# Expert results combined by one-hot products on TensorE instead of a round trip through DRAM, and the second branch's gate projections moved beside the first attention

## The chip, the cores and the metric

The kernel runs on one NeuronCore of a Trainium2 chip. The metric is the device time of one execution in microseconds (us), lower is better; 0.2% of it is about 4.4 us. PE is the matrix engine (TensorE), PEld its weight loads, DVE the vector engine, ACT the scalar engine, POOL the GpSimd engine, SP the engine that issues most DMAs.

## The reference, cut to what matters

All in float32, 256 tokens of width 1024, batch 1. Two blocks follow each other. The first one is a gated two-branch mixer followed by a mixture of experts:

```python
h = rmsnorm(x, norm1_g);  u, v_a, q, k, v_b = split(h @ w_in)
y_a = chunked_spatial_gating(u, v_a, ...)
o = diff_attention(q, k, vb, lam, slopes)          # 8 heads, two softmaxes each
y_b = rmsnorm(o, sub_norm_g) * 0.8
g_a, g_b = split(sigmoid(h @ w_gate + b_gate), 2)  # gates of both branches read h
x = x + (g_a * (y_a @ w_up_a) + g_b * (y_b @ w_up_b)) @ w_out

h2 = rmsnorm(x, norm2_g)
# 4 groups of 8 experts, top-2 of 8 inside the best group; per token two experts, two weights
x = x + sum over the two chosen experts e: weight_e * (silu(h2 @ w1[e]) * (h2 @ w3[e])) @ w2[e]
```

The second block has two layers. Each modulates x and a context stream ctx by vectors computed from c and ada_w (nine segments of 1024 per stream and layer), applies a feed-forward network (FFN) to both, then a mixer with attention, then a second FFN. The first FFN of the context stream reads ctx and the modulation alone, not x.

## The kernel before, in words

**Precision.** Most matrix products are done as three fp32r products: each operand is split into a high part (ACT copy, line 87 for weights) and the rest (DVE subtraction, line 88), and lines 121 to 123 issue high*high, high*low and low*high. Weight blocks are 128x1024 float32 (512 KB). `W` (line 76) loads one into a ring of raw tiles by an SP DMA (line 86), and splits it. The expert weights are used as plain fp32, with no split.

**Order of work.** The program is written as Python generators which are advanced step by step inside one another. A scheduler then fixes each engine's order ahead of time, from the program order and its own model of durations; on the chip each engine runs its list in that order.

**First block (`block1`, line 291).** The attention generator (line 418) yields 20 times: for each of two token tiles eight heads and two final transposes with splits into `ybT`. Beside it runs `merge(0, yaT)` (line 478), which has 16 steps: for each of eight column tiles d one gate step (24 matmuls of 256 columns, then a tanh on ACT) and one up step (24 matmuls, then a product on DVE into `mA`). Each attention step advances it by one. Each `W` call adds `self.rate` to a credit, and each whole credit pumps one step of the `ada` generator (line 820), which loads one modulation block (line 843) and after four of them runs `ada_rows` (lines 874 to 887: fp32 matmuls of line 880, small ones of line 885). After the attention `need(0, 1)` pumps the rest of the first 24 blocks, the context stream is normalised (`norm_hT`) into `cT`, and `merge(1, ybT)` runs 16 more steps, eight gate and eight up, into `mT`, which feeds w_out.

**Experts (`moe`, line 528).** A router picks two slots per token: 32 experts with 32 rows each (CAP), four experts to a group of 128 rows. `onehot(q)` builds for two groups at a time a 0/1 matrix tokens x rows; `gather` (line 684) multiplies the tokens by it, so each group gets its rows. For each of eight groups `first` (16 blocks of w13), `turn` and twice `second` (four blocks of w2 each, one for each half c of the columns) run; lines 704 are the fp32 matmuls of 32 rows. Raw expert blocks go through the same raw rings plus `araw` (13 tiles in all). Beside the experts, `steps` advances the FFN of the context stream (`ctx_steps`). `second` evicts its result (ACT, line 732) and writes it to a DRAM buffer `yo` by a POOL DMA (line 733). After the last group four indirect POOL DMAs (line 762) fetch each token's two rows, and DVE multiplies them by the weights and adds to x (line 763). Then come the remaining `ctx_steps`, and a conditional branch (line 768) for experts that got more than 32 rows, which all engines pass.

**Start of the second block (`block2`, line 1263).** `norm(0, 0, 0)` squares x (ACT, line 162), scales it (DVE, line 165), transposes (PE, line 127), modulates and splits it into `hT` (lines 220 to 222, 114, 115), and the first FFN starts. Its `W` calls pump the next modulation blocks; the first five of them have a DVE copy from x ahead of their load (line 842), so that they are not loaded before x is complete.

Of the kernel before, what the change touches and what calls it, by code (L numbers as in the profile page):

```python
# [6 lines left out]
F32 = mybir.dt.float32  # L7
F32R = mybir.dt.float32r
# [24 lines left out]
R2 = .3  # L33
# [13 lines left out]
class Builder:  # L47
# [243 lines left out]
    def block1(self):  # L291
        tc, nc, A = self.tc, self.nc, self.A
        x = self.x
        with tc.tile_pool(name="b1", bufs=1, reuse_waits="tile") as P:
# [183 lines left out]
            def merge(br, yT):  # L478
                for d2 in range(4):
                    wg = [self.W("w_gate", br * 8 + 2 * d2 + b) for b in range(2)]  # L480
                    wu = [self.W("w_up", br * 8 + 2 * d2 + b) for b in range(2)]
                    for c in range(2):
                        d = 2 * d2 + c
                        pg = self.mm([128, 256])
                        self.proj_T(pg, wg, c, hact)
                        gt = self.t(P, [128, 256], F32, "gt", 2)

                        nc.scalar.activation(out=gt, in_=pg, func=AF.Tanh, scale=0.5, bias=bg[:, br * 8 + d : br * 8 + d + 1])
                        yield
                        pu = self.mm([128, 256])  # L490
                        self.proj_T(pu, wu, c, lambda kt: (yT[:, 0, kt], yT[:, 1, kt]))
                        if br == 0:
                            nc.vector.scalar_tensor_tensor(out=mA[:, d], in0=gt, scalar=1.0, in1=pu, op0=OP.add, op1=OP.mult)
                        else:
                            nc.vector.scalar_tensor_tensor(out=gt, in0=gt, scalar=1.0, in1=pu, op0=OP.add, op1=OP.mult)
                            nc.vector.tensor_tensor(out=gt, in0=gt, in1=mA[:, d], op=OP.add)
                            hi, lo = mT[:, 0, d], mT[:, 1, d]
                            nc.scalar.activation(out=hi, in_=gt, func=AF.Copy, scale=0.5)
                            nc.vector.scalar_tensor_tensor(out=lo, in0=gt, scalar=0.5, in1=hi.bitcast(F32), op0=OP.mult, op1=OP.subtract)
                        yield  # L500

            self.rate = R2
            m0 = merge(0, yaT)
            for _ in attention():
                next(m0, None)
            for _ in m0:
                pass
# [8 lines left out]
            for _ in merge(1, ybT):  # L516
                pass
# [10 lines left out]
    def moe(self):  # L528
        tc, nc, A = self.tc, self.nc, self.A
        x = self.x  # L530
        with tc.tile_pool(name="moe", bufs=1, reuse_waits="tile") as P:
            self.xsp, self.xst = P, ("xg", 6)
# [3 lines left out]
            g2 = self.load_bc(P, "norm2_g", 1024, "xg", bufs=6)  # L536
# [14 lines left out]
            h2T = [self.t(P, [128, 4, 256], F32, "xg", 6) for _ in range(2)]  # L551
# [93 lines left out]
            sidx = s([128, 2, 2], "sidx", U32)  # L645
            nc.vector.tensor_copy(sidx, slot)
# [10 lines left out]
            yo = self.dr.tile([32 * CAP, 1024], F32, tag="yo", bufs=1, name="yo")  # L657
# [17 lines left out]
            def onehot(q):  # L675

                oh = self.t(P, [128, 2, 256], F32R, "oh", 2)
                for i in range(2):
                    t = self.t(P, [128, 256], F32, "oht", 1)
                    nc.vector.tensor_scalar(out=t, in0=iot, scalar1=sq[:, i, 0, q : q + 1], scalar2=None, op0=OP.is_equal)  # L680
                    nc.vector.scalar_tensor_tensor(out=oh[:, i], in0=iot, scalar=sq[:, i, 1, q : q + 1], in1=t, op0=OP.is_equal, op1=OP.add)
                return oh

            def gather(oh, k4):

                xg = self.t(P, [128, 4, 256], F32, "xg", 6)
# [81 lines left out]
            with tc.If(cnt > CAP):  # L768
                ctr = self.t(P, [128, 1], F32, "ctr")
                nc.vector.memset(ctr, 0.0)  # L770
                h2T = [self.t(P, [128, 4, 256], F32, "xg", 6) for _ in range(2)]
                for i in range(2):
                    h2 = self.t(P, [128, 1024], F32, "xg", 6)
# [6 lines left out]
                with tc.For_i(0, 32) as e:  # L780
                    pgu = [self.mm([128, 256], tag) for tag in ("mm", "mm", "at", "at")]
                    for b in range(4):
                        wf = self.t(P, [128, 1024], F32, "xg", 6)
# [14 lines left out]
                    for c in range(2):  # L798
                        wf = self.t(P, [128, 1024], F32, "xg", 6)
# [463 lines left out]
    def block2(self):  # L1263
        tc, nc, A = self.tc, self.nc, self.A
        x, ctx = self.x, self.ctx
        with tc.tile_pool(name="b2", bufs=1, reuse_waits="tile") as B:
# [31 lines left out]
            norm(0, 0, 0)  # L1298
            ffn(0, 1, [(stream(0, 0, 0),)] * 3, (0, 4, 8, 11), (x,))
# [182 lines left out]
```

## Time and profile before

| what | value |
|---|---|
| median of 3 runs (lowest to highest) | 2210.32 us (2210.27 to 2214.33) |
| the profiled execution, its time | 2208.52 us |
| the profiled execution, its span from first to last instruction | 2206.7 us |
| mean granted TensorE clock, share of full speed | 0.98 |
| PE busy | 2091.5 us, 95% |
| DVE busy | 1374.2 us, 62% |
| ACT busy | 876.6 us, 40% |
| HBM traffic | 206 GB/s over the span |

A share of busy time is an average over stages that have different limits. So the table says only that PE is nearly always occupied; which stage has slack is read from stretches of the trace. PE's matmuls overlap, so the time of one in the trace is longer than the distance from its start to that of the next: work on PE is priced by that distance.

### The profile page before, as it was taken

How to read it: one execution, taken by the hardware profiler on the slowest of the kernel's cores; microseconds unless marked ns; L12 is line 12 of the kernel's file. 1: busy time of each engine (PE TensorE's matmuls, PEld its weight loads, DVE VectorE, ACT ScalarE, POOL GpSimd, SP SyncE). 2: the span in 40 equal slices, each digit the busy share in tenths (PEclk: the TensorE clock that was granted, in tenths of full speed). 3: DMA queues.
4: the chain of work that ended last, by engine and by line, in shares of the span. 5: the costliest groups of instructions: out<-in, count | busy, mean ns of one | idle time of the engine just before them, and what ended most of it. 6: DMA issues, size and time to landing. Idle time of an engine off the chain costs nothing.

```text
span 2206.7 us, 31880 instructions
## 1 busy us (share of the span) xinstructions
PE 2091.5 (95%) x12314; PEld 1683.1 (76%) x12314; DVE 1374.2 (62%) x2480; ACT 876.6 (40%) x1372; POOL 58.4 (3%) x109
## 2 busy tenths in 40 slices
PE   7999999898886999999999999999999999888998
PEld 5888797545553888876787888888888888767997
DVE  5778576222324555476686848668766947866656
ACT  5556453222222544455563222245222224545443
POOL 1000000000001000010000000000000001000000
PEclk9999899999998999999999999999999999999999
DMA  8645665999999677742155636435644624505553
GB/s 315 209 164 179 213 225 203 356 403 393 408 398 354 212 269 256 260 177 68 53 191 187 219 105 200 151 127 180 192 164 133 221 97 149 171 20 167 187 190 116
DMA packets 126426, 456.87 MB, mean 207 GB/s; under 512 B 14960, under 2 KB 15104, under 8 KB 126144
## 3 DMA queue, kind: packets, MB, share of 16 engines
q1 hardware_dynamic: 118656, 431.02, 55.1%
q0 software_dynamic: 7616, 23.79, 3.3%
q8 instruction: 98, 1.61, 0.3%
q14 instruction: 56, 0.46, 0.1%
HBM read 448.41 MB, written 6.34 MB: 206 GB/s over the span
## 4 chain that ended last, share of the span: by engine, by line
PE 62%; DVE 2%; issue 1%; ACT 1%; DMA 1%; DVEq 0%; SPq 0%; ACTq 0%; POOLq 0%; POOL 0%
PE mm L121 12%; PE mm L122 12%; PE mm L123 12%; PE at L121 7%; PE at L123 7%; PE at L122 7%; PE tr L127 2%; PE ada L880 1%; PE ada L1148 1%; PE at L1127 1%; PE mm L1161 0%; ACT whi L87 0%; DMA araw<-ada_w 0%; PE ada L885 0%; DVE wlo L88 0%
## 5 line engine op out<-in xcount | busy, mean ns | idle before, releaser
L88 DVE TENSOR_TENSOR wlo<-raw,whi 128x1024 fp32r<-128x1024 f32 x410 | 501.2, 1223 | 347.0 <-ACT whi L87 341.7
L87 ACT ACTIVATE whi<-raw 128x1024 fp32r<-128x1024 f32 x410 | 434.5, 1060 | 613.4 <-PE at L122 156.3
L121 PE MATMUL mm<-hT,whi 128*128 128x256 f32 (+1 forms) x832 | 266.7, 323 | 0.5 <-ACT hT L114 0.3
L122 PE MATMUL mm<-hT,whi 128*128 128x256 f32 (+1 forms) x832 | 266.9, 322 | 0.2 <-DVE hT L115 0.2
L123 PE MATMUL mm<-hT,wlo 128*128 128x256 f32 (+1 forms) x832 | 266.3, 321 | 0.0
L122 PE MATMUL at<-hT,whi 128*128 128x256 f32 (+1 forms) x704 | 230.3, 328 | 0.0
L123 PE MATMUL at<-hT,wlo 128*128 128x256 f32 (+1 forms) x704 | 230.1, 328 | 0.0
L121 PE MATMUL at<-hT,whi 128*128 128x256 f32 (+1 forms) x704 | 229.8, 329 | 0.0
L121 PE MATMUL mm<-whi,fh 128*128 128x512 f32 x440 | 171.9, 399 | 8.1 <-ACT whi L87 7.8
L122 PE MATMUL mm<-wlo,fh 128*128 128x512 f32 x440 | 175.8, 400 | 3.0 <-DVE wlo L88 3.0
L123 PE MATMUL mm<-whi,fl 128*128 128x512 f32 x440 | 173.0, 398 | 0.0
L121 PEld LDWEIGHTS mm<-hT,whi 128*128 128x128 f32 x832 | 156.2, 189 | 16.5 <-ACT whi L87 1.2
L123 PEld LDWEIGHTS mm<-hT,wlo 128*128 128x128 f32 x832 | 157.0, 189 | 14.4 <-DVE xs L165 0.8
L122 PEld LDWEIGHTS mm<-hT,whi 128*128 128x128 f32 x832 | 157.0, 189 | 14.0 <-DVE hT L115 0.4
L121 PEld LDWEIGHTS at<-hT,whi 128*128 128x128 f32 x704 | 132.2, 189 | 15.8 <-ACT whi L87 0.8
L122 PEld LDWEIGHTS at<-hT,whi 128*128 128x128 f32 x704 | 132.5, 188 | 13.2
L123 PEld LDWEIGHTS at<-hT,wlo 128*128 128x128 f32 x704 | 132.4, 188 | 13.2
L88 DVE TENSOR_TENSOR wlo<-rawk,whi 128x1024 fp32r<-128x1024 f32 x72 | 88.1, 1223 | 74.8 <-ACT whi L87 74.3
L87 ACT ACTIVATE whi<-rawk 128x1024 fp32r<-128x1024 f32 x72 | 76.2, 1058 | 95.4 <-PE mm L123 39.5
L121 PEld LDWEIGHTS mm<-whi,fh 128*128 128x128 f32 x440 | 82.7, 189 | 35.7 <-ACT whi L87 13.3
L122 PEld LDWEIGHTS mm<-wlo,fh 128*128 128x128 f32 x440 | 83.5, 190 | 29.3 <-DVE wlo L88 6.4
L950 DVE TENSOR_TENSOR silu<-silu,at 128x256 f32<-128x256 f32 (+1 forms) x104 | 53.0, 510 | 79.7 <-PE at L123 77.0
(396 smaller groups left out, 4240.6 us busy)
## 6 DMA issues: line engine op xcount, KB each, us to landing
raw<-gu SPq DMA_DIRECT2D x214, 512.0 KB, 3.9
araw<-ada_w SPq DMA_DIRECT2D x144, 512.0 KB, 4.6
raw<-dn SPq DMA_DIRECT2D x108, 512.0 KB, 4.0
rawk<-w SPq DMA_DIRECT2D x65, 512.0 KB, 9.9
araw<-w SPq DMA_DIRECT2D x64, 512.0 KB, 9.9
raw<-w SPq DMA_DIRECT2D x63, 512.0 KB, 9.9
raw<-w_in SPq DMA_DIRECT2D x40, 512.0 KB, 4.6
raw<-w_out SPq DMA_DIRECT2D x28, 512.0 KB, 4.1
```

Source lines behind the costliest of these rows:

```text
L87: self.nc.scalar.activation(out=hi[:, :cols], in_=src, func=AF.Copy)
L88: self.nc.vector.tensor_tensor(out=lo[:, :cols], in0=src, in1=hi[:, :cols].bitcast(F32), op=OP.subtract)
L121: mm(p, lh, rh, start=first, stop=False)
L122: mm(p, lh, rl, start=False, stop=False)
L123: mm(p, ll, rh, start=False, stop=last)
L127: self.nc.tensor.transpose(out, in_, self.ident[:k, :k])
L880: nc.tensor.matmul(p[r], self.cc[:, kt], wf[kt // 2][:, kt % 2 * 512 : kt % 2 * 512 + 512], start=kt < 4, stop=kt >= 4)
L950: nc.vector.tensor_tensor(out=s, in0=s, in1=pgu[1][c], op=OP.mult)
L1127: nc.tensor.matmul(ps, d["qT"][tt][:, kv * 4 + hp], kT[kv][:, i, k0 * 128 : 512], start=(i == 0), stop=(i == 1))
L1148: nc.tensor.matmul(po[kv * 64 : kv * 64 + 64, hp], v[:, k0 + k, kv * 64 : kv * 64 + 64], aTs[kv][:, k], start=(k == 0), stop=(k == nk - 1))
```

## The change

1. In block1 the merge is cut into `gate` and `up`. Beside the attention now run the 16 steps of the first branch and then the eight gate steps of the second branch, 24 in all; their tanh results are kept in two tiles of the tag "T4" (four buffers, shared with the attention's output, the distance table and the context norm). After the context norm only the eight up steps of the second branch are left. The credit rate beside the attention goes from 0.3 to 0.34.
2. In moe the DRAM buffer `yo`, the index tile, 16 POOL writes, four indirect reads and four DVE additions are gone. `onehot` makes in addition the transposed 0/1 matrix (`ohT`) and each row's weight (`ws`). `second` evicts its result times `ws` as high part (ACT) and rest (DVE), multiplies both by `ohT` for the two token tiles on PE, and DVE adds the products to x.
3. Buffers: six "xg" tiles become five, the FFN of the context stream gets seven instead of eight hidden tiles.
4. After `norm(0, 0, 0)` the tile that holds back modulation loads is the last part of `hT`, no longer x.

```diff
-R2 = .3
+R2 = .34
...
+            gB = []
+            def gate(br, d2, put):
+                wg = [self.W("w_gate", br * 8 + 2 * d2 + b) for b in range(2)]
+                for c in range(2):
+                    d = 2 * d2 + c
+                    pg = self.mm([128, 256])
+                    self.proj_T(pg, wg, c, hact)
+                    nc.scalar.activation(out=put(d), in_=pg, func=AF.Tanh, scale=0.5, bias=bg[:, br * 8 + d : br * 8 + d + 1])
+                    yield
+            def up(br, d2, yT, gts, done):
+                wu = [self.W("w_up", br * 8 + 2 * d2 + b) for b in range(2)]
+                for c in range(2):
+                    d = 2 * d2 + c
+                    pu = self.mm([128, 256])
+                    self.proj_T(pu, wu, c, lambda kt: (yT[:, 0, kt], yT[:, 1, kt]))
+                    done(d, gts[d], pu)
+                    yield
...
                 for d2 in range(4):
+                    yield from gate(0, d2, put)
+                    yield from up(0, d2, yaT, gts, done)
+                for d2 in range(4):
+                    if d2 % 2 == 0:
+                        g = self.t(P, [128, 4, 256], F32, "T4", 4)
+                        gB.extend(g[:, i] for i in range(4))
+                    yield from gate(1, d2, lambda d: gB[d])
...
-            m0 = merge(0, yaT)
+            m = merge()
             for _ in attention():
-                next(m0, None)
+                next(m, None)
...
-            for _ in merge(1, ybT):
-                pass
+            for d2 in range(4):
+                for _ in up(1, d2, ybT, gB, add):
+                    pass
...
-            ctx_steps = self.ffn(P, 0, 1, [(sc,)] * 4, CUT)
+            ctx_steps = self.ffn(P, 0, 1, [(sc,)] * 4, CUT, nb=7)
...
-            sidx = s([128, 2, 2], "sidx", U32)
-            nc.vector.tensor_copy(sidx, slot)
...
-            yo = self.dr.tile([32 * CAP, 1024], F32, tag="yo", bufs=1, name="yo")
...
             def onehot(q):
                 oh = self.t(P, [128, 2, 256], F32R, "oh", 2)
+                wo = self.t(P, [128, 2, 256], F32, "wo", 1)
                 for i in range(2):
...
+                    nc.vector.tensor_scalar(out=t, in0=t, scalar1=win[:, i, 0:1], scalar2=None, op0=OP.mult)
+                    nc.vector.tensor_scalar(out=wo[:, i], in0=iot, scalar1=sq[:, i, 1, q : q + 1], scalar2=win[:, i, 1:2], op0=OP.is_equal, op1=OP.mult)
+                    nc.vector.tensor_tensor(out=wo[:, i], in0=wo[:, i], in1=t, op=OP.add)
+                for n in range(2):
+                    c = slice(n * 128, n * 128 + 128)
+                    p = self.mm([128, 2, 128], "tr")
+                    for i in range(2):
+                        self.tr(p[:, i], oh[:, i, c].bitcast(F32))
+                    ohT = self.t(P, [128, 2, 128], F32R, "ohT", 4)
+                    nc.scalar.activation(out=ohT, in_=p, func=AF.Copy)
+                    p = self.mm([128, 1], "tr")
+                    for i in range(2):
+                        nc.tensor.matmul(p, wo[:, i, c], ones[:, 0:1], start=(i == 0), stop=(i == 1))
+                    ws = self.t(P, [128, 1], F32, "ws", 4)
+                    nc.vector.tensor_copy(ws, p)
+                    back[2 * q + n] = ohT, ws
...
-                os = self.t(P, [128, 512], F32, "os", 2)
-                nc.scalar.activation(out=os, in_=pO, func=AF.Copy)
-                nc.gpsimd.dma_start(yo[g * 128 : g * 128 + 128, c * 512 : c * 512 + 512], os)
+                ohT, ws = back[g]
+                oh_, ol = (self.t(P, [128, 512], F32R, n, 2) for n in ("os", "ol"))
+                nc.scalar.activation(out=oh_, in_=pO, func=AF.Copy, scale=ws)
+                nc.vector.scalar_tensor_tensor(out=ol, in0=pO, scalar=ws, in1=oh_.bitcast(F32), op0=OP.mult, op1=OP.subtract)
+                for tt in range(2):
+                    p = self.mm([128, 512], "tr")
+                    nc.tensor.matmul(p, ohT[:, tt], oh_, start=True, stop=False)
+                    nc.tensor.matmul(p, ohT[:, tt], ol, start=False, stop=True)
+                    xs_ = x[:, tt, c * 512 : c * 512 + 512]
+                    nc.vector.tensor_tensor(out=xs_, in0=p, in1=xs_, op=OP.add)
...
-            for i in range(2):
-                for j in range(2):
-                    yg = self.t(P, [128, 1024], F32, "xg", 6)
-                    nc.gpsimd.indirect_dma_start(out=yg, out_offset=None, in_=yo, in_offset=bass.IndirectOffsetOnAxis(ap=sidx[:, i, j : j + 1], axis=0))
-                    nc.vector.scalar_tensor_tensor(out=x[:, i], in0=yg, scalar=win[:, i, j : j + 1], in1=x[:, i], op0=OP.mult, op1=OP.add)
-
             steps(None)
...
             norm(0, 0, 0)
+            self.gate = T[:, 0, 1, 7].bitcast(F32)
```

## Rows read from the trace of the kernel before

**Rows 1.** The page's head and its part 1.

```profile
span 2206.7 us, 31880 instructions
PE 2091.5 (95%) x12314; PEld 1683.1 (76%) x12314; DVE 1374.2 (62%) x2480; ACT 876.6 (40%) x1372; POOL 58.4 (3%) x109
```

**Rows 2.** Windows: length, busy us (instructions) per engine, clock, DMA share, GB/s.

```profile
145.00:206.50 61.50, 61.50 (x514) 57.99 (x513) 51.84 (x129) 37.72 (x92) 0.00 (x0) 1.00 0.43 146
206.50:234.60 28.10, 21.28 (x114) 12.95 (x112) 19.07 (x68) 12.27 (x33) 0.53 (x1) 0.70 0.57 206
265.00:270.00 5.00, 5.00 (x47) 5.00 (x46) 2.03 (x5) 0.78 (x2) 0.00 (x0) 1.00 0.91 331
...
420.00:680.00 260.00, 225.15 (x1401) 134.35 (x1400) 72.13 (x89) 63.08 (x91) 7.05 (x13) 0.97 1.01 402
676.00:693.30 17.30, 16.75 (x88) 10.93 (x87) 9.70 (x11) 7.11 (x8) 2.35 (x3) 1.00 0.85 307
693.30:719.60 26.30, 8.82 (x38) 3.21 (x37) 14.10 (x34) 4.93 (x8) 5.43 (x6) 0.68 0.95 350
```

**Rows 3.** Groups by line, PE alone, 206.5 to 234.6 us.

```profile
L880 PE MATMUL ada<-araw,cc 128*32 128x512 f32 x40 | 7.1, 839 | 2.1 <-ACT hft L459 2.1
L453 PE MATMUL ada<-A,aT 128*128 128x128 f32 x24 | 5.5, 392 | 1.3 <-ACT aT L451 1.1 <-DVE acols L887 0.3
L885 PE MATMUL ada<-csel,araw 128*128 128x2 f32 x16 | 3.5, 343 | 1.2 <-ACT araw L882 1.2
L127 PE MATMUL tr<-ident,T 128*128 128x128 f32 x12 | 2.6, 379 | 0.0
L127 PE MATMUL tr<-ident,e 128*128 128x128 f32 x10 | 2.3, 314 | 2.2 <-DVE rsy L141 1.1 <-DVE r L444 1.1
```

**Rows 4.** Chain of waits: pieces of PE work at full clock (start, us, what).

```profile
774.93 1.85 PE ada L880 x16
782.11 0.79 PE ada L885 x8
...
1036.97 0.59 PE tr L127 x4
```

**Rows 5.** DMA queues, 380 to 680 us: packets, MB, share of 16 engines.

```profile
q1 hardware_dynamic: 31354, 114.17, 96.0%
q0 software_dynamic: 1120, 3.67, 3.0%
```

**Rows 6.** Groups by line, 380 to 680 us: evictions of 128x512.

```profile
L901 DVE TENSOR_TENSOR gadd<-mm,grow 128x512 f32<-128x512 f32 x9 | 6.2, 692 | 23.1 <-PE mm L123 22.7
L732 ACT ACTIVATE os<-mm 128x512 f32<-128x512 f32 x14 | 8.4, 597 | 60.6 <-PE mm L704 60.6
```

**Rows 7.** Timeline of PE at the end of the experts (start, us, what).

```profile
692.76 0.39 PE L122 MATMUL mm<-wlo,fh 128*128 128x512 f32 x1
692.99 0.39 PE L123 MATMUL mm<-whi,fl 128*128 128x512 f32 x1
710.16 3.79 PE L880 MATMUL ada<-araw,cc 128*32 128x512 f32 x8 [16.79 <-DMA araw<-ada_w]
...
719.57 0.49 PE L121 MATMUL mm<-hT,whi 128*128 128x256 f32 x2
```

**Rows 8.** Timelines of DVE, ACT, SP and POOL over the same stretch.

```profile
696.49 0.68 DVE L902 TENSOR_TENSOR A<-A,gadd 128x512 f32<-128x512 f32 x1
...
705.03 1.28 DVE L763 SCALAR_TENSOR_TENSOR x<-xg,win,x 128x1024 f32<-128x1024 f32 x1 [0.88 <-DMA xg<-yo,sidx]
...
711.17 0.75 DVE L165 TENSOR_SCALAR xs<-x,rsy 128x1024 f32<-128x1024 f32 x1
...
706.41 1.06 ACT L162 ACTIVATE xs<-x 128x1024 f32<-128x1024 f32 x1 [11.94 <-DVEq L768]
...
682.42 14.50 SPq L86 DMA_DIRECT2D raw<-gu  x8
...
691.83 1.26 POOL L762 DMA_INDIRECT xg<-yo,sidx  x1 [6.16 <-DMA yo<-os]
```

More of the change, by code (lines that the diff above doesn't have):

```diff
@@ L476, in block1 @@
             mT = None
-            def merge(br, yT):
-                for d2 in range(4):
[L480 to L500, printed above, removed]
@@ new lines, in merge, with put, done @@
+            def merge():
+                gts = {}
+                def put(d):
+                    gts[d] = self.t(P, [128, 256], F32, "gt", 2)
+                    return gts[d]
+                def done(d, gt, pu):
+                    nc.vector.scalar_tensor_tensor(out=mA[:, d], in0=gt, scalar=1.0, in1=pu, op0=OP.add, op1=OP.mult)
+                for d2 in range(4):
+                    yield from gate(0, d2, put)
[5 more added lines that the diff above has]
+                    yield from gate(1, d2, lambda d: gB[d])
@@ new lines, in add @@
+            def add(d, gt, pu):
+                t = self.t(P, [128, 256], F32, "gt", 2)
+                nc.vector.scalar_tensor_tensor(out=t, in0=gt, scalar=1.0, in1=pu, op0=OP.add, op1=OP.mult)
+                nc.vector.tensor_tensor(out=t, in0=t, in1=mA[:, d], op=OP.add)
+                hi, lo = mT[:, 0, d], mT[:, 1, d]
+                nc.scalar.activation(out=hi, in_=t, func=AF.Copy, scale=0.5)
+                nc.vector.scalar_tensor_tensor(out=lo, in0=t, scalar=0.5, in1=hi.bitcast(F32), op0=OP.mult, op1=OP.subtract)
@@ L502, in block1 @@
             self.rate = R2
-            m0 = merge(0, yaT)
+            m = merge()
             for _ in attention():
-                next(m0, None)
-            for _ in m0:
+                next(m, None)
+            for _ in m:
                 pass
@@ L550, in moe @@
             h2l = self.t(P, [128, 2, 1024], F32R, "h2l")
-            h2T = [self.t(P, [128, 4, 256], F32, "xg", 6) for _ in range(2)]
+            h2T = [self.t(P, [128, 4, 256], F32, "xg", 5) for _ in range(2)]
             for i in range(2):
@@ L681, in onehot @@
                     nc.vector.scalar_tensor_tensor(out=oh[:, i], in0=iot, scalar=sq[:, i, 1, q : q + 1], in1=t, op0=OP.is_equal, op1=OP.add)
+                    nc.vector.tensor_scalar(out=t, in0=t, scalar1=win[:, i, 0:1], scalar2=None, op0=OP.mult)
[14 more added lines that the diff above has]
+                    back[2 * q + n] = ohT, ws
                 return oh
+            back = {}
             def gather(oh, k4):
-                xg = self.t(P, [128, 4, 256], F32, "xg", 6)
+                xg = self.t(P, [128, 4, 256], F32, "xg", 5)
                 for k2 in range(2):
@@ L770, in moe @@
                 nc.vector.memset(ctr, 0.0)
-                h2T = [self.t(P, [128, 4, 256], F32, "xg", 6) for _ in range(2)]
+                h2T = [self.t(P, [128, 4, 256], F32, "xg", 5) for _ in range(2)]
                 for i in range(2):
-                    h2 = self.t(P, [128, 1024], F32, "xg", 6)
+                    h2 = self.t(P, [128, 1024], F32, "xg", 5)
                     nc.vector.tensor_tensor(out=h2, in0=h2h[:, i].bitcast(F32), in1=h2l[:, i].bitcast(F32), op=OP.add)
@@ L782, in moe @@
                     for b in range(4):
-                        wf = self.t(P, [128, 1024], F32, "xg", 6)
+                        wf = self.t(P, [128, 1024], F32, "xg", 5)
                         nc.sync.dma_start(wf, A["w13"].rearrange("(e b) p c -> e b p c", b=4)[e, b])
@@ L798, in moe @@
                     for c in range(2):
-                        wf = self.t(P, [128, 1024], F32, "xg", 6)
+                        wf = self.t(P, [128, 1024], F32, "xg", 5)
                         nc.sync.dma_start(wf, A["w2"].rearrange("(e b) p c -> e b p c", b=2)[e, c])
```

4 lines of the change are left out of this document (2 added, 2 removed).

## The prediction

> **What bounds the kernel now.** The page says that PE is busy for 95% of the span [rows 1], but that share counts a matmul's modelled end and a slow clock as work, so I read stretches. Windows around the two edits give five different pictures [rows 2]. From 145 to 206.5 us, attention with the first branch's merge beside it, PE is busy throughout at full clock: bound by PE. From 206.5 to 234.6 us the sixteen merge steps are used up and the attention runs alone: the granted clock is 0.70 on average and only 114 matmuls are issued, against 47 in 5 us in a stretch full of merge work. From 420 to 680 us the experts run at 402 GB/s with the DMA share at 1.01 while PE has 34.85 us without work: bound by the weight stream. From 676 to 693.3 us PE finishes the context FFN. From 693.3 to 719.6 us PE is busy for 8.8 of 26.3 us: a chain of waits. Before the edits and after them PE is bound by its own work, so a microsecond won in these stretches moves everything behind it.
>
> **Part 1, the gate steps.** The change removes no PE work; it moves eight gate steps. A step is 24 matmuls; at 47 in 5 us [rows 2] that is 2.55 us, so 20.4 us of work become available as filler. What is there to fill? The work in the 28.1 us by kind [rows 3], priced at distances of full-clock pieces [rows 4]: 40 of line 880 at 1.85/16 = 0.116 us are 4.6; 16 of line 885 at 0.79/8 = 0.10 are 1.6; 22 transposes at 0.59/4 = 0.15 are 3.2; 24 of line 453 have no piece of their own and get 0.15 as the same tile size, 3.5; the twelve others left of the 114 at 0.15 are 1.8. That is 14.7 us, so 13.4 us are idle time or slow clock. The filler exceeds it, but the list of each engine is fixed ahead, and the attention's small matmuls now queue behind gate matmuls, as they did until 206.5 us. Four gate steps fall beside the last four attention yields, four behind them; there they cover the normalisation and transposes that lead to the up steps. I take 12 us; bounds 4 (the tail is only half covered) and 13.4.
>
> What else moves with it. The same weight loads are issued, eight of them earlier, into a stretch with a DMA share of 0.57 [rows 2]: hidden. The higher rate shifts four modulation blocks of 512 KB on SP's queue, and one call of line 880's routine, from behind the attention to the gate steps: the same work in the same stretch, nothing. The two gate tiles take two of the four T4 buffers, so the context norm's second tile must wait until the attention's output is transposed. Behind it wait the context transposes, which nobody needs before the context FFN; eight up steps (20.4 us) cover this. If that cover failed, the norm's own chain of some 5 us would show.
>
> **Part 2, the expert stretch.** Removed: yo writes. In 380 to 680 us fourteen of the sixteen sit in the POOL queue's share, 3.0% of 300 us, or 9.0 us of all DMA engines [rows 5]; since the stream is the bound there, that is the gain if PE keeps up. The index copy and POOL's issuing go too, for nothing, since nobody waits on either.
>
> Added on PE: per `second` four fp32r matmuls of 512 columns, 0.23 us apart [rows 7], 64 in all: 14.7 us. Per `onehot` four transposes at 0.15 and four pairs of tiny products at most at line 885's 0.10 per instruction, two each: 4 x (0.6 + 0.8) = 5.6 us. Together 20.3 us. Added elsewhere: per `second` one DVE eviction and two additions of 128x512, 0.69 each [rows 6], 33 us, plus in all 24 operations of 128x256 for the one-hot weights, at most 0.69 each, on a DVE that is busy for 72 of 260 us [rows 2]: hidden, except that PE waits for them. ACT's eviction stays the same size.
>
> PE's 34.85 us without work exceed 20.3, and thirteen raw tiles let the stream run ahead; but PE does not idle evenly. I charge a quarter, 5 us, of the added work as pauses of the stream. Bounds: nothing, and all of it with waits, priced under the rivals. The two products of the last group come when the stream is over and PE is the bound (the window from 676 us, [rows 2]); they cost 8 x 0.23 = 1.8 us. Net: 9 - 5 - 1.8 = 2 us; bounds +9 and -32. I stay near the upper end because the nearest row, PE's free time in this stretch, covers the work. Five xg tiles hold a group's two, the next two and one more; seven hidden tiles hold a part's six and the first of the next part, while the following one comes four weight blocks later. Both cost nothing, the cover being the 10 us of PE work of four blocks.
>
> **Part 3, between the last expert and the next FFN.** Now PE issues its last context matmul at 692.99 us [rows 7]. DVE finishes the context additions at 697.17, then waits for the four indirect reads, the first of which had itself waited for the last yo write, and ends the last addition at 706.31 [rows 8]. ACT's first square of x waits for DVE to pass the branch [rows 8]. With the reads gone x has long been complete, and what is late next is the context addition: the square starts at about 697.3, 9.1 us earlier. From the square the scaled second tile takes until 711.92 [rows 8], as now. Then the first FFN matmul came 7.65 us later, because one group of line 880, its loads let in by x, stood ahead of the transposes, slow and spread out by its loads: 3.79 us for eight [rows 7] where full clock gives 0.93 [rows 4]. With the new gate tile those loads wait until `norm` is done. What is left is a transpose piece, two halves of a modulation and a split, about 2.8 us, so 4.85 us more. The group comes back inside the FFN as 1.85 + 0.79 = 2.64 us [rows 4].
>
> Who is queued behind the new wait: a DVE copy, then the five modulation loads on SP, then later FFN weights. Eight weight blocks were issued before 697 us [rows 8], and a block is another 24 matmuls, so 20.4 us of FFN work cover it.
>
> The clock: PE rests for 16.8 us [rows 7] and the granted clock averages 0.68 over the stretch [rows 2], so part of it is at 1.2 GHz; now line 880's group takes that part. In the new order the FFN's first matmuls do. If as long a piece as those 3.79 us runs at half speed, about 2 us are lost; I take them. The Trainium skill, "TensorE: Matmul & The Clock Gate", section "What's actually happening", says that the throttled clock is the default and activity releases it; by that rule the moved group was a warm-up that the change throws away, and the trace agrees in that the group ran slow and the FFN behind it did not. Without this rule the part would give 11.3 us, with it 9.3.
>
> Part 3: 9.1 + 4.85 - 2.64 - 2 = 9.3 us, I say 9.
>
> **Sum.** 12 + 2 + 9 = 23 us. The profiled execution took 2208.5 us (span 2206.7), the median of the runs is 2210.3, 1.8 above it. So 2185.5 profiled and 2187 as the median.
>
> **Rivals.**
> - *The combine becomes PE's wait (slower).* At each `second` PE reaches the combine before its operands are there and stands for 0.60 + 0.69 = 1.3 us [rows 6]: 16 x 1.3 = 21 us, with 20 us of added work 41. If none is absorbed by PE's free time, less 9 for the writes, the experts lose 32 us; parts 1 and 3 bring 21: 11 slower, 2221. It decides from an exposure of 30 us on. For it: PE is in order, and the stream halts when thirteen tiles are full. Against: other matmuls are ready, 34.85 us are free. Chance 0.06.
> - *Half of that:* 21 us exposed; the experts lose 12, the total gain is 9: 2201. Chance 0.11.
> - *The writes cost the stream nothing,* because they fill gaps: then the 9 us do not come, gain 14, 2196. Against: the share stands at 1.01. Chance 0.08.
> - *x's norm still starts late,* because its new tiles lie where the context stream is being copied out to DRAM, a copy issued behind the context addition. Then part 3 gives about 1 us: 2195. Chance 0.09.
> - *The gate steps do not fill the hole,* since the fixed order puts them behind the attention after all (the change would not do what it says): part 1 gives 0 to 4, 2195 to 2199. Chance 0.08.
> - Two of these together end within 0.2% of the old time: 0.05.
> - *Everything goes through:* part 1 13.4, part 2 7, part 3 11, 31 us, 2179; the order shuffled elsewhere may add or take a few. Inside the forecast's own spread.
>
> **Numbers.** The forecast has 0.53: 2187. A measurement of this kernel can tell about 0.2%, 4.4 us, from no change. Faster by more: 0.53 + 0.11 + 0.08 + 0.09 + 0.08 = 0.89; same 0.05; slower 0.06. The range reaches from the best case with 8 us of shuffling, 2171, to the half-exposed combine, 2203; it leaves out the two cases above and the edges.
>
> **What would show it.** Right: in the stretch behind the sixteenth merge step the clock stays at 1.00 and the context norm's transposes lie among up steps; no POOL writes among the experts and a stream near 420 GB/s; the 13.4 us between the last context matmul and the square of x become about 4, and no line 880 stands ahead of the first FFN matmul. Wrong: PE waiting for the DVE eviction of the combine in the list of waits, SP waiting for PE longer than now, or gate matmuls in one block behind the attention.

## The result and the profile after

The changed kernel takes 2186.6 us (median of 4 runs, 2184.1 to 2187.45) where the kernel before took 2210.3 (4 runs, 2209.43 to 2214.33): a ratio of 0.9893, 95% interval 0.9874 to 0.9912. The forecast was 2187. The total is right, but not all of its parts are: one part fell short by about as much as a stretch far behind the change won unforeseen. The span fell from 2206.7 [rows 1] to 2184.7 us:

```profile
span 2184.7 us, 32131 instructions
PE 2100.7 (96%) x12426; PEld 1692.7 (77%) x12426; DVE 1408.3 (64%) x2555; ACT 879.5 (40%) x1380; POOL 44.6 (2%) x89
```

Windows of the kernel after, columns as in [rows 2]; the first has the same place, the others are moved to where the same work now stands:

```profile
206.50:234.60 28.10, 27.36 (x218) 24.13 (x217) 21.52 (x58) 18.11 (x41) 0.53 (x1) 1.00 0.61 218
318.00:322.00 4.00, 4.00 (x24) 4.00 (x24) 1.85 (x14) 0.59 (x2) 0.00 (x0) 0.61 0.31 121
413.40:673.40 260.00, 240.14 (x1513) 143.35 (x1512) 104.33 (x151) 65.97 (x99) 0.00 (x0) 0.99 0.97 382
687.60:700.20 12.60, 3.40 (x15) 2.22 (x13) 8.39 (x25) 4.44 (x7) 1.99 (x3) 0.63 0.65 218
```

The attention's tail is full: 218 matmuls at full clock where 114 stood. Between the experts and the next FFN 12.6 us are left of 26.3. But the expert stretch moves 382 GB/s where it moved 402, at a DMA share of 0.97 instead of 1.01: it did not speed up when the writes went. The timelines of PE and ACT at the end of the experts, kernel after:

```profile
687.61 0.40 PE L123 MATMUL mm<-whi,fl 128*128 128x512 f32 x1
...
691.91 1.06 ACT L162 ACTIVATE xs<-x 128x1024 f32<-128x1024 f32 x1 [2.81 <-DVEq L811]
...
696.21 1.08 PE L127 MATMUL tr<-ident,xs 128*128 128x128 f32 x4 [8.21 <-DVE rsy L151]
...
700.17 0.78 PE L121 MATMUL mm<-hT,whi 128*128 128x256 f32 x2
...
703.52 0.41 PE L123 MATMUL at<-hT,wlo 128*128 128x256 f32 x1
703.73 0.41 PE L121 MATMUL at<-hT,whi 128*128 128x256 f32 x1
```

From the last context matmul to the square of x it is 4.3 us instead of 13.4, and no modulation group stands ahead of the first FFN matmul any more [rows 7, 8]. That FFN begins slowly: its matmuls are 0.21 us apart, and from 704.59 us on 0.12.

To see where time goes I read, in every trace, the start of the same events. The kernels besides before and after are the experiments described below. "poolc" are the pooling matrices of the second block's mixer in its first layer (layer 0), and "fftw" is an operand of a product that comes later in it. The first line is the kernel before (us); below it, how much earlier each event comes:

| kernel | w_out's last addition | first expert matmul | last expert matmul | last context addition | first square of x | first FFN matmul | first addition of that FFN to x | mixer: first with poolc | mixer: first fftw | last addition to x |
|---|---|---|---|---|---|---|---|---|---|---|
| before | 307.1 | 365.3 | 683.5 | 696.5 | 706.4 | 719.6 | 786.5 | 1013.0 | 1045.0 | 2197.9 |
| after | 11.2 | 6.5 | 6.6 | 5.5 | 14.5 | 19.4 | 15.1 | 15.1 | 21.4 | 22.1 |
| after_again | 10.4 | 7.3 | 5.4 | 4.3 | 13.3 | 18.2 | 14.6 | 14.3 | 20.7 | 22.0 |
| p1_gates | 11.9 | 11.8 | 12.5 | 12.5 | 12.7 | 12.2 | 14.2 | 10.4 | 7.6 | 7.9 |
| p2_combine | -0.2 | -3.3 | -4.0 | -5.1 | 3.9 | 0.6 | -0.1 | 2.0 | 5.2 | 4.2 |
| p3_gate | 4.3 | 4.3 | 0.6 | 0.6 | -0.1 | 4.8 | 0.9 | 0.0 | 6.8 | 4.9 |
| no_gate | 12.3 | 9.2 | 9.4 | 8.3 | 17.3 | 14.0 | 13.9 | 10.5 | 13.6 | 10.2 |
| yo_kept | 12.0 | 8.9 | 4.5 | 3.4 | 12.4 | 17.3 | 13.2 | 13.1 | 19.7 | 20.8 |
| no_combine | 12.2 | 12.0 | 22.6 | 22.6 | 31.6 | 36.5 | 33.6 | 31.1 | 31.1 | 32.8 |
| one_product | 12.1 | 9.0 | 19.2 | 18.6 | 27.2 | 32.1 | 28.2 | 26.9 | 29.6 | 29.9 |
| high_twice | 12.6 | 9.5 | 16.3 | 15.2 | 23.9 | 28.8 | 24.8 | 22.1 | 23.7 | 24.5 |
| late_combine | 11.6 | 6.9 | 6.9 | 5.8 | 14.8 | 19.7 | 15.3 | 14.9 | 18.9 | 19.7 |
| turn_late | 11.1 | 7.1 | 2.8 | 1.7 | 10.7 | 15.6 | 12.0 | 11.6 | 14.4 | 15.1 |
| before_mc3 | -0.5 | -0.5 | 1.4 | 1.4 | 0.3 | 0.5 | 0.6 | 1.8 | 5.1 | 0.1 |

A difference between neighbouring columns is what a stretch won or lost. One line is one execution. p3_gate's program differs from the kernel before only behind the experts, yet it is 4.3 us earlier by the first column, and its expert stretch (first to last expert matmul) takes 321.9 us where before had 318.2. The four kernels with the writes and without the combine (before, p1_gates, p3_gate, before_mc3) took 316.2 to 321.9 us there, so a single trace is good to some 4 us over such a stretch. ("The 32-row products" of the expectations below are those of the column "first fftw", 128x256 in shape; the words were wrong, the instruction is the same.)

### The profile page after: what moved, and what is told of

It is laid out like the page before. It is cut to its first block, busy times and chain, and to the rows that moved or that the text cites. A ratio compares the mean times of both kernels' runs of the same rounds, so it can differ in the third digit from the quotient of the medians.

```text
span 2184.7 us, 32131 instructions
## 1 busy us (share of the span) xinstructions
PE 2100.7 (96%) x12426; PEld 1692.7 (77%) x12426; DVE 1408.3 (64%) x2555; ACT 879.5 (40%) x1380; POOL 44.6 (2%) x89
## 4 chain that ended last, share of the span: by engine, by line
PE 63%; DVE 2%; issue 1%; ACT 1%; DMA 0%; DVEq 0%; ACTq 0%; POOLq 0%; POOL 0%
PE mm L121 12%; PE mm L122 12%; PE mm L123 12%; PE at L121 7%; PE at L122 7%; PE at L123 7%; PE tr L127 2%; PE ada L923 1%; PE ada L1191 1%; PE at L1170 1%; PE ada L928 0%; PE mm L1204 0%; ACT whi L87 0%; DVE wlo L88 0%; PE mm L1240 0%
## 5 line engine op out<-in xcount | busy, mean ns | idle before, releaser
L123 PEld LDWEIGHTS mm<-hT,wlo 128*128 128x128 f32 x832 | 157.8, 190 | 14.4 <-issue 0.8
L122 PEld LDWEIGHTS at<-hT,whi 128*128 128x128 f32 x704 | 133.5, 190 | 13.2
L123 PEld LDWEIGHTS at<-hT,wlo 128*128 128x128 f32 x704 | 133.2, 189 | 13.2
L894 DVE SCALAR_TENSOR_TENSOR araw<-araw 128x1024 f32<-128x1024 f32 x72 | 88.0, 1222 | 21.7 <-DMA araw<-ada_w 20.1
```

What stands on the lines that cost most here:

```text
L122: mm(p, lh, rl, start=False, stop=False)
L123: mm(p, ll, rh, start=False, stop=last)
L894: nc.vector.scalar_tensor_tensor(out=jk, in0=raw, scalar=1.0, in1=cb[1], op0=OP.mult, op1=OP.mult, accum_out=cols[:, 1, n : n + 1])
```

## The experiments

### Each part by itself

`p1_gates` is the kernel before with point 1 of the change; `p2_combine` with points 2 and 3; `p3_gate` with point 4; `no_gate` is the kernel after without point 4:

```diff
--- p3_gate against before; no_gate takes the same line out of after
             norm(0, 0, 0)
+            self.gate = T[:, 0, 1, 7].bitcast(F32)
--- p1_gates against before
-R2 = .3
+R2 = .34
...
-            m0 = merge(0, yaT)
+            m = merge()
             for _ in attention():
-                next(m0, None)
+                next(m, None)
...
--- p2_combine against before
-                nc.gpsimd.dma_start(yo[g * 128 : g * 128 + 128, c * 512 : c * 512 + 512], os)
...
+                nc.scalar.activation(out=oh_, in_=pO, func=AF.Copy, scale=ws)
...
+                    nc.tensor.matmul(p, ohT[:, tt], oh_, start=True, stop=False)
+                    nc.tensor.matmul(p, ohT[:, tt], ol, start=False, stop=True)
...
```

> The kernel before with the gate steps alone moved (and the rate R2 .34); experts, yo and the part in front of the first FFN as before. Theory (the gate steps fill the attention's tail and nothing else depends on it): last addition of w_out into x some 11 us earlier (before: 307.1), and the same 11 us at every later landmark, so about 2199 us. Rival (the layer-0 mixer's 6 us come from the shift in time of everything in front of it): 11 us up to the first FFN, then 17 at the end of the mixer, 2193. Second rival (the router stretch loses part of the gain by the order of the context FFN's steps, whatever the combine does): first expert matmul only 6 to 7 us earlier, about 2203.

Measured: 2200.7 us, ratio 0.9956 (0.9936 to 0.9976). The theory holds up to the first FFN: 11.9 us at w_out's last addition, 11.8 at the first expert matmul, 12.2 at the first FFN matmul, and 14.2 at its first addition to x. Then the mixer takes 6.6 us back between that and "first fftw". Both rivals fall: the mixer did not win by the shift, it lost; and the loss ahead of the experts in the kernel after is not the gate steps', since p1_gates loses 0.1 us there.

> The kernel before with the combine on TensorE alone (yo and the indirect reads gone, 5 xg and 7 hidden tiles), no gate step moved, no new gate tile in front of the FFN. Theory (the added work in front of and among the experts uses up what the writes give back, and the gain lies in x's norm behind the experts): first expert matmul 2 to 5 us later than 365.3, expert stretch 315 as before, square of x about 4 to 9 us earlier than 706.4, first FFN matmul earlier by less, since the line-880 group is still ahead of it: in all 0 to 7 us faster, 2203 to 2210. Rival (the 4.7 us lost ahead of the experts come from the moved gate steps, not from the combine): first expert matmul at 365, total 2198 to 2203.

Measured: 2205.6 us, ratio 0.9986 (0.997 to 1.0003). The theory holds nearly number by number (its "315 as before" for the expert stretch should have read 318): 3.1 us lost ahead of the first expert matmul, 0.7 in the stretch, 1.1 behind it, 9.0 won at the square of x, and 3.4 of these lost again before the first FFN matmul. By the first addition to x the combine alone is worth nothing. The timeline of PE in p2_combine shows why its 9 us shrink:

```profile
709.24 1.92 PE L897 MATMUL ada<-araw,cc 128*32 128x512 f32 x4 [10.66 <-DMA araw<-ada_w]
719.01 0.50 PE L121 MATMUL mm<-hT,whi 128*128 128x256 f32 x2
```

x is ready earlier, but the group of line 880 of the kernel before (897 here) still stands ahead of the transposes and waits for its loads.

> The kernel before with the one line that takes the modulation loads behind the first norm, nothing else. By the prediction's terms: first FFN matmul 4.85 us earlier, 2.64 us given back inside the FFN and 2 by the clock, so 0 to 1 us faster, 2209 to 2211. Rival (the moved group warms the clock and its place is free): no difference at the first FFN matmul, slower by 2 to 3 us behind it. If the late poolc load of the layer-0 mixer hangs on the order of these loads, the mixer's end comes a further 6 us earlier: 2203.

Measured: 2204.1 us, ratio 0.9979 (0.9966 to 0.9992). 4.9 us earlier from the square of x to the first FFN matmul, of which 3.9 go back inside the FFN: the prediction's 4.85 less 2.64 and 2, as far as one trace can tell. The time is 0.2% under before, and the 5.9 us that its mixer wins (first addition to x to "first fftw") are more than all of that.

> The kernel after without the line that takes the modulation loads behind the first norm. By the prediction's terms: square of x as in the kernel after (691.9), first FFN matmul some 5 us later than its 700.2, and 2.6 + 2 us not given back in the FFN: within 2 us of the kernel after, 2185 to 2188. Rival (the line, by the order of the loads, is also what removes the layer-0 mixer's wait for poolc): 6 us slower than the kernel after, 2192 to 2194, the loss lying between 940 and 1060 us.

Measured: 2201.3 us, ratio 0.9968 (0.9954 to 0.9982), outside the theory's 2185 to 2188 and past the rival's 2192 to 2194. From the last context addition to the first addition to x it wins 5.6 us where the kernel after wins 9.6; so with the combine the line is worth 4 us, alone (p3_gate) 0.3. The rest of the difference to the kernel after lies in the mixer and behind it: it keeps 10.2 of 13.9 us where after makes 22.1 of 15.1.

Put together, the parts add up as far as the first addition to x: 14.2 - 0.1 + 0.9 = 15.0 us for the three alone, 15.1 in the kernel after, and 14.1 for points 1 to 3, where no_gate has 13.9. (That it comes out to 0.2 us is more than single executions can promise.) Behind it they don't: from there to the last addition to x p1_gates loses 6.3 us, no_gate 3.7, p2_combine wins 4.3, p3_gate 4.0 and the kernel after 7.0. So the medians don't add up either: the three alone are 7.3, 2.4 and 4.0 us under the kernel before that ran beside them, 13.7 together, where the kernel after is 23.7 and, once more, 20.6 under it.

### The kernel after once more

> The kernel after, unchanged, once more and beside the experiments: how far does one execution's trace repeat? If the landmarks are set by the order of the work, each comes within 1 us of the first trace (w_out's last addition 295.3, first expert matmul 358.8, first FFN matmul 700.2, first addition to x 771.4, the mixer's 32-row products from 1023.6). If the 6 us in the mixer are a matter of when transfers happen to meet, the last one moves by several us while the others stay. Time 2182 to 2190.

Measured: 2186.6 us (2185.1 to 2187.7), ratio 0.9902 (0.9874 to 0.993). All landmarks repeat within 1.3 us, the mixer's gain too (6.1 us between the first addition to x and "first fftw", 6.3 in the first trace). So the mixer's gain comes with this order of instructions and is no accident of one execution. One thing did not repeat: in the window 318 to 322 us (above) the clock was 0.61, here

```profile
318.00:322.00 4.00, 4.00 (x37) 4.00 (x37) 2.01 (x10) 1.27 (x4) 0.00 (x0) 1.00 0.36 131
```

37 matmuls instead of 24. The slow clock accounts for 1.5 of the 4.7 us that the kernel after lost there; the six kernels with the combine and without that slow clock lose 3.1 each.

### What the writes and the combine cost the stream

```diff
--- yo_kept against after
...
+                nc.gpsimd.dma_start(yo[g * 128 : g * 128 + 128, c * 512 : c * 512 + 512], oh_.bitcast(F32))
--- no_combine against after
...
-                    back[2 * q + n] = ohT, ws
...
-                    nc.tensor.matmul(p, ohT[:, tt], oh_, start=True, stop=False)
-                    nc.tensor.matmul(p, ohT[:, tt], ol, start=False, stop=True)
-                    xs_ = x[:, tt, c * 512 : c * 512 + 512]
-                    nc.vector.tensor_tensor(out=xs_, in0=p, in1=xs_, op=OP.add)
...
+                nc.scalar.activation(out=oh_, in_=pO, func=AF.Copy)
```

> The kernel after with the sixteen writes of the expert results to DRAM put back on POOL's queue (of the rounded high part; nobody reads them). Theory of the prediction (the DMA share is the bound of the expert stretch, and the writes take 9 us of it): from the first expert matmul to the last second's 9 us more than in the kernel after, 327 instead of 318 by its first and last expert matmul, time 2194 to 2196. Rival (the stretch is set by PE and by the buffers that PE frees, the writes fill gaps): 318 to 320, time within 3 us of the kernel after.

Measured: 2186.2 us (two executions), ratio 0.99 (0.9863 to 0.9937): the time of the kernel after. The stretch took 322.6 us against 318.1 and 320.1 in two executions without the writes; at the last expert matmul it is 0.9 to 2.1 us behind them. With the combine in place the writes cost some 1 to 4.5 us, not 9; the stretch fits neither theory, the time the rival's.

> The kernel after without the combine: no transposed one-hot, no weights, no products, no addition to x (x gets no expert result at all) and no writes to DRAM either; ACT still evicts. Theory (the 9 us of the writes are there but the added PE work eats them): first expert matmul some 5 us earlier than in the kernel after, expert stretch 306 to 309 instead of 318. Rival (the writes never cost the stream anything, the added work neither): first expert matmul earlier, expert stretch 318 all the same or longer by what the earlier start gives.

Measured: 2176.8 us (two executions), ratio 0.9858 (0.9822 to 0.9894). The theory holds: first expert matmul 5.4 us earlier than after, and a stretch of 307.5 us instead of 318.1. Against p1_gates, which has the writes and no combine (317.5), the writes are worth 10.0 us; against the four such kernels, 8.7 to 14.4. The windows from the first to the last expert matmul, in the kernel before and in no_combine:

```profile
365.30:683.50 318.20, 281.17 (x1813) 170.58 (x1813) 95.06 (x123) 79.61 (x116) 7.69 (x15) 0.97 0.98 387
```

```profile
353.35:660.87 307.52, 280.03 (x1814) 169.94 (x1814) 95.19 (x123) 79.21 (x116) 0.00 (x0) 0.97 0.97 388
```

PE has the same work in both (1813 and 1814 matmuls). Without the writes it stands idle for 27.5 us instead of 37.0: the time of the writes was part of PE's idle time. The waits of PE between 360 and 676 us tell what it waits for (us in total, times, longest). Before, for weights (line 87 splits a weight block of the context FFN, and ACT there waits for the block's load):

```profile
PE mm L121 <- ACT whi L87: 15.1, 9, 2.6
PE at L704 <- DMA rawk<-w: 6.3, 8, 1.6
PE at L704 <- DMA raw<-w: 3.4, 10, 0.9
```

and after, with the combine's wait for its eviction:

```profile
PE mm L121 <- ACT whi L87: 9.4, 6, 2.6
PE tr L780 <- ACT os L775: 7.2, 9, 0.9
PE at L746 <- DMA araw<-w: 0.8, 1, 0.8
PE at L746 <- DMA rawk<-w: 0.6, 2, 0.4
PE at L746 <- DMA raw<-w: 0.2, 1, 0.2
```

Before, PE waited 10 us for expert weights and 15 for splits; after, 1.6 and 9.4, and 7.2 for evictions. The stream was the bound and had the writes on it. After, what PE waits for is in good part the combine itself, and the stretch is just as long. That PE and its evictions are now the longer of the two bounds is read from this list and from yo_kept; the stream has not let go of PE altogether. In no_combine PE waits for weights again:

```profile
PE mm L121 <- ACT whi L87: 11.5, 8, 2.6
PE at L729 <- DMA raw<-w: 3.1, 7, 1.3
PE at L729 <- DMA rawk<-w: 2.9, 7, 1.3
```

### Which part of the combine it is

```diff
--- one_product against after (high_twice takes out the first line alone and has oh_ for ol in the second)
...
-                nc.vector.scalar_tensor_tensor(out=ol, in0=pO, scalar=ws, in1=oh_.bitcast(F32), op0=OP.mult, op1=OP.subtract)
...
-                    nc.tensor.matmul(p, ohT[:, tt], ol, start=False, stop=True)
...
--- late_combine against after
...
                     if g and 0 < b < 3:
-                        second(g - 1, hd, b - 1)
+                        late, now = second(g - 1, hd, b - 1), late
...
+                    if now:
+                        combine(*now)
...
--- turn_late against after
...
-            oh = onehot(0)
+            oh, wo = onehot(0)
             xg = [gather(oh, k4) for k4 in range(2)]
+            turned(0, oh, wo)
...
```

> The kernel after with only the product of the rounded high part; the residual of its rounding to fp32r and the product with it are left out (so the combine rounds the expert results): 32 matmuls of 512 columns (7.4 us) and 16 DVE operations fewer. Theory (the expert stretch, 318 to 320 us by its first and last matmul, is set by PE's work once the combine is in it): 4 to 7 us shorter. Rival (it is set by the chain of waits eviction, product, addition, whose length stays): within 2 us of the kernel after.

Measured: 2183.4 us (2178.7 to 2187.3; the profiled one is the fastest), ratio 0.9897 (0.988 to 0.9914). The stretch took 308.0 us, 10.1 less than after: more than the theory's 4 to 7 and the 7.4 us of the matmuls, and it is where no_combine has its floor. So half of the combine costs the stretch next to nothing and the other half 10 us, which fits a stretch that takes the longer of two bounds, as far as single executions can tell.

> The kernel after without the residual of the rounding (its sixteen DVE operations are left out), but with as many products as in the kernel after: the high part is multiplied twice, so x gets each expert result doubled. Theory (PE's added matmuls set the expert stretch): 316 to 320 us by its first and last expert matmul, as with both parts, where the single product had 308. Rival (DVE's extra eviction, which PE's products wait for, sets it): 308 to 310.

Measured: 2186.6 us, ratio 0.9902 (0.9885 to 0.9918), stretch 311.3 us: between the two. It leaves the residual out and adds every expert result to x twice. Windows from the first to the last expert matmul of one_product, high_twice and the kernel after:

```profile
356.33:664.30 307.97, 280.22 (x1876) 173.02 (x1876) 116.12 (x169) 82.25 (x123) 0.00 (x0) 0.98 0.97 388
```

```profile
355.86:667.18 311.32, 284.11 (x1905) 177.54 (x1904) 116.05 (x169) 82.15 (x123) 0.00 (x0) 0.98 0.97 383
```

```profile
358.79:676.89 318.10, 293.38 (x1905) 175.86 (x1904) 126.78 (x184) 82.20 (x123) 0.00 (x0) 0.98 0.95 375
```

Against one_product, as many matmuls as in the kernel after cost 3.3 us; DVE's residual with its place in the chain costs the other 6.8. Neither theory has it alone, and with single executions good to some 4 us the split is not settled. By the timed runs the residual is worth nothing that can be told (high_twice and after_again are both at 2186.6).

> The kernel after with each combine's products and additions written one block of weights later, so that ACT's and DVE's evictions are done when PE comes to them. Theory (PE stands for the evictions, 7.2 us in the kernel after, and that is half of what the combine costs the expert stretch): stretch 4 to 7 us shorter than 318 to 320. Rival (PE's added work sets it, where it stands is of no matter): within 2 us, with that wait gone from the list.

Measured: 2187.4 us, ratio 0.9912 (0.9894 to 0.9931), stretch 318.2. It tests nothing: in the trace PE's list through the experts has the combine's products where the kernel after has them. PE's wait is the same to the tenth:

```profile
PE tr L783 <- ACT os L775: 7.2, 9, 0.9
```

Whether a combine moved one block back would help stays open.

> The kernel after with the transposed one-hot and its weights made behind the gather of the group's tokens instead of ahead of it. Theory (the first expert waits for the added one-hot work that stands ahead of the first gather): first expert matmul 2 to 4 us earlier than 358.8, the same gain at the last second. Rival (what is lost there is DVE's five operations, which stay ahead of the gather, or the weight stream): first expert matmul within 1 us of 358.8, or earlier without a gain at the last second.

Measured: 2193.3 us, ratio 0.9932 (0.9907 to 0.9957). First expert matmul at 358.3, 0.5 us earlier than after (both with the slow clock at 318 us), and the stretch 322.4. The trace has the transposes behind the gather now. The rival: PE's transposes in front of the gather are not what costs. What is left of the 3.1 us ahead of the experts (DVE's operations, or context steps that run earlier in the new order) was not separated.

### The mixer

```diff
--- before_mc3 against before
-MC = 2
+MC = 3
```

> The kernel before with three buffers instead of two for the pooling matrices of the layer-0 mixer (the load of the third needs no wait for a product). Theory (the mixer's loss of some 6 us in the kernel before is PE's wait for that load and the slow clock after it): no wait for poolc in the trace, from the first product with poolc to the first of the 32-row products that follow about 26 us as in the kernel after instead of 32, time 5 to 7 us under the kernel before. Rival (the stretch is as long for another reason, the order of other matmuls in it): wait gone, stretch 30 to 32 us, time within 3 us of the kernel before.

Measured: 2208.1 us, ratio 1.0003 (0.999 to 1.0016). The wait was not gone: with three buffers PE waits at the next load. Timelines of PE, the longest wait for poolc in before, before_mc3, p1_gates and after:

```profile
1022.19 1.97 PE L1161 MATMUL mm<-poolc,pf 128*64 128x256 f32 x4 [2.69 <-DMA poolc<-c_pool]
```

```profile
1020.60 1.57 PE L1161 MATMUL mm<-poolc,pf 128*64 128x256 f32 x4 [2.02 <-DMA poolc<-c_pool]
```

```profile
1012.11 1.97 PE L1187 MATMUL mm<-poolc,pf 128*64 128x256 f32 x4 [2.96 <-DMA poolc<-c_pool]
```

```profile
1003.06 0.65 PE L1204 MATMUL mm<-poolc,pf 128*64 128x256 f32 x2 [0.65 <-DMA poolc<-c_pool]
```

The piece from the first poolc product to the first fftw product took 32.0 us before, 28.8 with three buffers, 34.8 in p1_gates and 25.7 after. A slow clock can follow the wait, as in this window of p1_gates; in high_twice, with a wait of 2.59 us, none does (1.00 over its piece):

```profile
1010.00:1020.00 10.00, 7.89 (x26) 4.13 (x26) 2.23 (x8) 1.51 (x6) 0.54 (x1) 0.54 0.18 70
```

So long waits for poolc and long pieces go together, but the 3.3 us that three buffers win are gone by the end of the kernel. Nor does the piece hold the same work in every kernel. Before and after:

```profile
1012.99:1045.03 32.04, 29.24 (x178) 18.52 (x178) 20.23 (x62) 15.69 (x50) 3.26 (x6) 0.95 0.34 106
```

```profile
997.88:1023.60 25.72, 24.71 (x153) 15.78 (x153) 16.88 (x53) 14.27 (x45) 3.28 (x6) 1.00 0.34 113
```

Of the 6.3 us between these two, 2.0 are the shorter wait and some 1.6 the clock (0.95 against 1.00 over 32 us); the rest goes with 25 matmuls that stand elsewhere, and what they cost there was not read. That the load is the cause of the 6 us is not shown; that the piece's length and its contents depend on the order of the instructions, which any edit here shuffles, is (25.2 to 34.8 us over these kernels).

## Why the prediction was right in its total, and where not

- **Part 1, 12 us: right.** 11.2 us in the kernel after, 11.9 alone, for the reason given: clock 1.00 and 218 matmuls in the stretch. How much of the 13.4 us was clock and how much idle the prediction left open; p3_gate, the same program there, shows the same window at

```profile
206.50:234.60 28.10, 20.73 (x134) 11.09 (x132) 20.10 (x68) 13.81 (x36) 0.53 (x1) 0.94 0.69 245
```

  with a clock of 0.94 instead of 0.70. The same 179 matmuls around it take 33.2 us there (from 206.56) and 36.9 before (from 207.12). So 3.7 of the 13.4 us went with a slow clock that one of four executions of this stretch had for a shorter time.
- **Part 2, net +2 us: wrong.** Measured: -4.7 ahead of the experts, 0.1 in the stretch, -1.1 behind it (forecast -1.8): -5.7. The step that failed is "I charge a quarter, 5 us, of the added work as pauses of the stream": the combine cost the stretch 10.6 us (no_combine against after; 12.6 against after_again). The 9 us of the writes were sized right, 10.0 by no_combine against p1_gates, but they can't be had beside the combine. I set PE's 34.85 us without work against 20.3 us of additions as if idle time were a store to draw on, and booked the writes' 9 us beside it; but those 9 us were part of that idle time, so they were counted twice (37.0 us idle in the stretch with the writes, 27.5 without). Of the 27.5, the combine filled no more than 2.8: in the kernel after PE is busy for 13.4 us more and still idle for 24.7 us, among it 7.2 us of a new wait, for evictions. The longer of two bounds counts, and the shorter was only some 10 us away. The prediction's own signs say so too: the stream moved 382 GB/s and not near 420, and a wait for the combine's eviction is in the list, though for ACT's and not DVE's. Second, nothing was charged ahead of the first expert matmul, where the one-hot work of the first group stands ahead of its gather: 3.1 us in six kernels, of what exactly stays open.
- **Part 3, 9 us: right, 9.6.** Square of x 9.0 us earlier over the last context addition (forecast 9.1), first FFN matmul another 4.9 (4.85), 4.3 given back in the FFN (4.64). What I missed is that the two are not separate terms: without the new gate tile 3.3 us of the 9 are lost to the group's loads. The clock: with the group ahead of it the FFN of no_gate has the full clock from its first matmul (1.00 from 705.6 to 710 us); in the kernel after it begins at half of it,

```profile
700.17:704.59 4.42, 4.42 (x23) 4.42 (x22) 2.35 (x4) 1.60 (x3) 0.00 (x0) 0.50 0.83 339
```

  so that some 2.2 of these 4.4 us are lost, where the forecast took 2. The Trainium skill ("TensorE: Matmul & The Clock Gate", "What's actually happening") says that activity releases the throttle. This trace agrees: PE had stood without work for 8.21 us ahead of the transposes, the products behind them began at 0.50, and from 704.59 to 710 us the clock is 1.00.
- **Not foreseen: +6.3 us in the mixer,** 300 us behind the change. It made up for part 2: 11.2 - 5.7 + 9.6 = 15.1 us up to the first addition to x, plus 6.3 there, plus 0.7 behind it, is 22.1; forecast 23. That the total came out is luck: by its parts as measured up to there the prediction would have said 15 us, 2195, and other orders of the mixer's same work lose where this one wins (p1_gates 6.6 us).
- **The rivals.** "The combine becomes PE's wait" had the mechanism right and the size too large: 14.8 us were exposed (10.6 in the stretch, 3.1 ahead of it, 1.1 behind it), between the forecast's 6.8 and the 21 of the case "half of that", and a wait of the products for the evictions stands in the list (7.2 us). "The writes cost the stream nothing" is refuted without the combine and nearly right with it (1 to 4.5 us). The gate steps filled the hole, and x's norm did not start late.

None of these versions that keeps the whole computation beats the kernel after. one_product's 2183.4 us can't be told from it by its interval.

## What to carry to other kernels

Where a transfer is taken off a saturated stream and paid for with work on the other engine, work out both bounds for the new stretch and take the longer; don't book the transfer's share as a gain and discount the work by idle time, for the idle time holds that share already. Test such a trade with a kernel that drops the transfer and the new work both: the floor it shows (307.5 us here) says what the trade leaves on the table. And fill a thin stretch first: it was the safest term here, and it repeated in every kernel that had it (10.4 to 12.6 us). A stretch that no edit touches can still change with the order of the instructions: give a forecast room for it, and count the instructions between two landmarks before a difference there is put down to anything.

## What the runs showed of the hardware that was not expected

- The granted clock can fall while PE has work without a gap: in the kernel after it was 1.00 from 312 to 318 us and 0.61 from 318 to 322 us, with PE busy all the time, from 315.5 us on with 32 products of the router of 36 columns each among those of 256. At the same place late_combine and turn_late had 0.83 from 316 to 326 us, as the kernel after; after_again, the same program as after, had 1.00. The cause stays open.
- The same thin stretch (206.5 to 234.6 us, no gate steps in it) was granted 0.66, 0.70, 0.70 and 0.94 in four executions, and 0.94 against 0.70 went with 3.7 us; with the gate steps it was 1.00 in all ten. The kernel before scatters by 12 us (2202.4 to 2214.1 in 24 runs on one chip), the kernel after by 4 (2184.1 to 2187.7 in eight). The thin stretch is not all of that: no_gate has it filled and scatters by 8.
